# Queries stored by rows and turned by transposing DMAs, keys held as their high part twice with the low part passed through memory: one transformer layer on one Trainium2 core

## The chip, the core and the metric

The kernel is one program on one core of a Trainium2 chip. The core has a matrix engine (TensorE, PE in the profile, with its weight loads as PEld), a vector engine (VectorE, DVE), an activation engine (ScalarE, ACT), a general engine (GpSimd, POOL) and a queue engine (SyncE, SP), which here issues nearly every DMA. Each engine works through its own instructions in the order in which they were written and waits on semaphores for the others. All DMAs of the core share 16 DMA engines. SBUF is the on-chip memory, 128 partitions wide; PSUM is the small memory into which TensorE writes.

The metric is the device time of one execution in microseconds (us): less is better.

## The reference, cut to what matters

The layer takes 2048 latent rows and 256 context rows of width 1024. It normalises them, projects them with `w_in` to retention inputs (rq, rk, rv, rg) and attention inputs (aq, ak, av), runs a bidirectional retention and a dense attention side by side, projects both back with `w_out`, and ends with a squared-ReLU feed-forward part and a norm. What the change touches is the attention's queries and keys:

```
rq, rk, rv, rg, aq, ak, av = jnp.split(h @ w_in, SPLIT_IDX, axis=-1)
q = _apply_rope(_rmsnorm(aq.reshape(B, L, ATT_HEADS, ATT_HD), q_norm_g), *att_cs)
k = _apply_rope(_rmsnorm(ak.reshape(B, L, ATT_KV_HEADS, ATT_HD), k_norm_g), *att_cs)
kc = _rmsnorm(cak.reshape(B, Lc, ATT_KV_HEADS, ATT_HD), k_norm_g)
...
def _dense_attention(q, k, v):
    s = jnp.einsum('bqkgd,bskd->bkgqs', q, k).astype(jnp.float32) * ATT_SCALE
    p = jax.nn.softmax(s, axis=-1).astype(v.dtype)
    return jnp.einsum('bkgqs,bskd->bqkgd', p, v)
```

There are 8 query heads of width 64 and 2 key heads, so each key head serves a group of 4 query heads. The keys are 256 context rows and 2048 latent rows.

## The kernel before

**Stages.** The program has three stages, one after the other. The first (us 0 to 605 of the profile) normalises the rows and makes all projections; it writes the finished pieces to scratch tensors in device memory. The second (605 to about 1450) runs attention, the retention and the output projection woven together. The third is the feed-forward part.

**Float32 through two half-width parts.** TensorE multiplies float16 here, so most operands are split into a high part (the value rounded to float16) and a low part (what the rounding left), and a product is the sum of high times high, high times low and low times high. For scores that is done inside one matmul of 128 rows: a head is only 64 wide, so the 128 rows of a tile hold two things of 64 rows each.

**The layout of the scores before.** `ks` (line 138) holds, for each of the 2 key heads and all 2304 keys, the high part of the keys on rows 0 to 63 and the low part on rows 64 to 127. A query tile `qr` (128 x 2 x 4 x 128: a first half x = 0 and a second half x = 1, 4 heads, 128 queries) holds in half 0 the high part of the queries twice, so that `ks` against half 0 gives (key high + key low) x query high. Half 1 holds the low part of the queries on rows 0 to 63, and rows 64 to 95 are overwritten with the row maxima (line 204). `ks2` (lines 1520 to 1523) holds the high part of the keys on rows 0 to 63 and a constant pattern `unit` on rows 64 to 127, so that `ks2` against half 1 gives key high x query low and subtracts the maximum. `scores` (line 206) does both matmuls for a block of 128 keys; `piece` (line 172) does matmuls with `ks` and half 0 alone, from which `maximum` (line 183) takes the row maxima beforehand.

**The order of the first stage.** The projections are cut into units: one unit is one tile of 128 rows times one block of columns (RQ, RK, RV, RG, AQ of 512 columns, AKV of 256). The list (line 1186) goes through two groups of row tiles: first 2 context and 4 latent tiles, each kind of column after the other, then the other 12 latent tiles with the blocks [RV], [RK, AKV], [AQ, RQ], [RG], in which the two kinds of a block alternate. Unit s has 24 matmuls (lines 1192 to 1194). What follows on a unit is written with `do(step, part, function)` (line 307), and `run_step(s)` (line 310) issues, right after the matmuls of unit s, all that was put down for step s, in this order of parts: hi, evac, turned, low, vec, pool, root, aux, turn, load, store. So the order on each engine and on SP's queue is written out by hand, and an instruction put down for a later step stands behind all those of the earlier ones on its engine.

**A query unit (AQ, lines 763 to 789).** Step +1: ACT copies it from PSUM (`xs`). Steps +2 and +3: norm and rotary embedding on DVE and POOL give `ys`. Step +4, part turn: TensorE turns the 128 x 512 float32 tile with four transposes (line 711) into a PSUM tile `psx`. Step +5: ACT copies it as float16 (the high part, line 782), and DVE subtracts (the low part, line 785), both into `qhl`. That tile is of the ring `zs` of two buffers, which the turned RQ and RK tiles share (line 739). Step +6: SP stores it to the scratch `aq` (line 789).

**A key unit (AKV, lines 790 to 842).** Step +4: ACT copies the key as float16 (`kh`, line 829). Step +5: DVE subtracts, so that `kn` holds the key and its low part side by side in float32 (line 832). Step +6: TensorE turns both (line 837). Step +7, part vec: DVE copies the turned tile into `ks` as float16 (line 842). There are 18 key tiles.

**Loading the queries.** One attention group is one tile of 128 queries and one key head: 32 groups, in the order of the list `order` (line 266). `Group.load` (lines 157 to 164) fetches its `qr` by four DMAs of 64 KB, each from 64 rows of `aq` to 64 partitions. The first two groups are loaded during the first stage (lines 1280 and 1281, part store of fixed steps), and their pieces run there too: group 0's pieces stand in the middle of the units' matmuls (line 1489). In the second stage time goes by events k; a group has 18 of them, its load stands 14 events before its first piece (line 1569), and SP issues it in the phase dma.

Of the kernel before, what the change touches and what calls it, by code (L numbers as in the profile page):

```python
# [13 lines left out]
F16 = mybir.dt.float16  # L14
# [42 lines left out]
def layer_kernel(ctx: ExitStack, tc: tile.TileContext, a: dict, out: bass.AP):  # L57
# [31 lines left out]
    rk_d = scratch("rk", NK, [P, 512])  # L89
    rv_d = scratch("rv", NK, [P, 512])  # L90
    rg_d = scratch("rg", NT, [P, 512])
    aq_d = scratch("aq", NT, [P, 2, 4, P], F16)
    qt_d = scratch("qt", NT, [P, 512])
    kt_d = scratch("kt", NT, [P, 512])
    av_d = dram.tile([P, 2, NK, HD], F32, name="av", tag="av")
# [53 lines left out]
    class Group:  # L149
# [7 lines left out]
        def load(self):  # L157
            pool, tag = (mq, "mb") if self.n % 4 < 2 else (qp, "qr")
            self.qr = pool.tile([P, 2, 4, P], F16, name="qr", tag=tag, bufs=2)
            q = self.qr.rearrange("p x (j e) t -> p x j e t", e=2)  # L160
            for e in range(2):
                src = aq_d[self.t][64 * e : 64 * e + 64, :, 2 * self.g : 2 * self.g + 2]
                nc.sync.dma_start(q[:64, :, :, e], src)
                nc.sync.dma_start(q[64:, :, :, e], src)

        def minima(self, pool):
            if pool is None:
# [102 lines left out]
    with ExitStack() as st, tc.manual_schedule():  # L270
# [418 lines left out]
        def post(s, g, col, kind, i, x):  # L689

            row = i if kind == "c" else i + NC
            scale = RSC if col == C_RK else 1.0
            if g:
                n = 3 if col == C_RK else 4 if col == C_RG else 2
                scale = sci[:, n : n + 1]

            def evac(func=AF.Copy, width=512):
                x["x"] = new("xs", "xs", 3)
                nc.scalar.activation(x["x"][:, :width], x["ps"][:, :width], func, scale=scale)

            def new_y():
                x["y"] = new("ys", "ys", 3)
                return x["y"]

            def heads(v, h):
                return v.rearrange("p (h d) -> p h d", h=h)

            def turn():
                x["pt"] = psT.tile([P, 4, P], F32, name="psx", tag="psx")
                for h in range(4):  # L710
                    nc.tensor.transpose(x["pt"][:, h], x["y"][:, h * P : (h + 1) * P], ident)

            if col in (C_RQ, C_RK):
                do(s + 1, "evac", evac)
                if kind == "c":
                    do(s + 2, "store", lambda: nc.sync.dma_start(rk_d[row], x["x"]))
                    return

                def load():
                    x["tb"] = op.tile([P, 2, P], F32, name="rtb", tag="rtb", bufs=3)  # L720
                    nc.sync.dma_start(x["tb"], a["ret_cs"][i * P : (i + 1) * P])

                do(s, "load", load)
                rope(
                    s + 2,
                    x,
                    lambda: heads(new_y(), H),
                    lambda: heads(x["x"], H),
                    lambda: x["tb"][:, 0],
                    lambda: x["tb"][:, 1],  # L730
                    H,
                    CH,
                )
                if col == C_RK:
                    do(s + 4, "store", lambda: nc.sync.dma_start(rk_d[row], x["y"]))
                dst = qt_d[i] if col == C_RQ else kt_d[i]

                def turned():
                    x["z"] = op.tile([P, 4, P], F32, name="zs", tag="zs")
                    nc.scalar.activation(x["z"], x["pt"], AF.Copy)  # L740

                late = s + 4 + (s < 5)
                do(late, "turn", turn)
                do(late + 1, "turned", turned)
                do(late + 2, "store", lambda: nc.sync.dma_start(dst.rearrange("p (h t) -> p h t", h=H), x["z"]))
            elif col == C_RV:
                do(s + 1, "evac", evac)
                do(s + 2, "store", lambda: nc.sync.dma_start(rv_d[row], x["x"]))
            elif col == C_RG:

                def gated():
                    nc.gpsimd.tensor_tensor(new_y(), x["x"], gnb, op=ALU.mult)

                def greatest():
                    nc.vector.tensor_reduce(
                        wmx[:, 72 + i : 73 + i], x["y"], axis=AX.X, op=ALU.max, apply_absolute_value=True
                    )

                do(s + 1, "evac", evac, AF.Silu)
                do(s + 2, "pool", gated)  # L760
                do(s + 3, "vec", greatest)
                do(s + 3, "store", lambda: nc.sync.dma_start(rg_d[i], x["y"]))
            elif col == C_AQ:
                att_tables(s, x, i)
                do(s + 1, "evac", evac)
                head_norm(s + 1, x, 8, "q", scale)
                rope(
                    s + 2,
                    x,
                    lambda: heads(new_y(), 8),  # L770
                    lambda: heads(x["x"], 8),
                    lambda: x["tb"][:, 0, 0],
                    lambda: x["tb"][:, 0, 1],
                    8,
                    HD,
                    lambda: bc(x["r"].unsqueeze(2), [P, 8, HD]),
                )
                do(s + 4, "turn", turn)

                def high():  # L780
                    x["z"] = op.tile([P, 2, 4, P], F16, name="qhl", tag="zs")
                    nc.scalar.activation(x["z"][:, 0], x["pt"], AF.Copy)

                def low():
                    nc.vector.tensor_tensor(x["z"][:, 1], x["pt"], x["z"][:, 0], op=ALU.subtract)

                do(s + 5, "turned", high)
                do(s + 5, "vec", low)
                do(s + 6, "store", lambda: nc.sync.dma_start(aq_d[i], x["z"]))
            else:  # L790
                do(s + 1, "evac", evac, AF.Copy, 256)
                src = lambda: x["x"][:, 128:256].rearrange("p (g d) -> p g d", g=2)
                do(s + 2, "store", lambda: nc.sync.dma_start(av_d[:, :, row], src()))
                head_norm(s + 1, x, 2, "k", scale)

                def new_k():
                    x["kn"] = op.tile([P, 2, 2, HD], F32, name="kn", tag="kn", bufs=4)
                    return x["kn"][:, :, 0]

                r = lambda: bc(x["r"].unsqueeze(2), [P, 2, HD])  # L800
                if kind == "c":

                    def plain():
                        w = bc(g2[:, 1, 0].unsqueeze(1), [P, 2, HD])
                        nc.gpsimd.tensor_tensor(new_k(), heads(x["x"][:, :128], 2), w, op=ALU.mult)

                    do(s + 2, "pool", plain)
                    do(
                        s + 3,
                        "vec",  # L810
                        lambda: nc.vector.tensor_tensor(x["kn"][:, :, 0], x["kn"][:, :, 0], r(), op=ALU.mult),
                    )
                else:
                    att_tables(s, x, i)
                    rope(
                        s + 2,
                        x,
                        new_k,
                        lambda: heads(x["x"][:, :128], 2),
                        lambda: x["tb"][:, 1, 0],  # L820
                        lambda: x["tb"][:, 1, 1],
                        2,
                        HD,
                        r,
                    )

                def high():
                    x["kh"] = op.tile([P, 2, HD], F16, name="kh", tag="kh")
                    nc.scalar.activation(x["kh"], x["kn"][:, :, 0], AF.Copy)

                def low():
                    nc.vector.tensor_tensor(x["kn"][:, :, 1], x["kn"][:, :, 0], x["kh"], op=ALU.subtract)

                def turn_k():
                    x["pt"] = psT.tile([P, 4, P], F32, name="psx", tag="psx")
                    for g in range(2):
                        nc.tensor.transpose(x["pt"][:, g], x["kn"][:, g].rearrange("p a b -> p (a b)"), ident)

                do(s + 4, "hi", high)
                do(s + 5, "low", low)  # L840
                do(s + 6, "turn", turn_k)
                do(s + 7, "vec", lambda: nc.vector.tensor_copy(ks[:, :, row * P : (row + 1) * P], x["pt"][:, :2]))

        def value_parts(s):

# [673 lines left out]

    ks2 = vp.tile([P, 2, NK * P], F16, name="ks2")  # L1520
    for g in range(2):
        nc.sync.dma_start(ks2[:64, g], ks[:64, g])
        nc.sync.dma_start(ks2[64:, g], a["unit"])
    mts = [vp.tile([P, 4, 32], F16, name=f"mt{i}") for i in range(2)]
    for mt in mts:
# [961 lines left out]
```

## Time and profile before

| What | Value |
|---|---|
| median of 3 runs | 2648.01 us (2645.45 to 2649.12) |
| the profiled execution: its own time | 2648.93 us |
| the profiled execution: its span, first to last instruction | 2647.1 us |
| mean granted TensorE clock | 0.997 |
| bytes moved by DMA | 481.84 MB, mean 182 GB/s |
| the 64 + 64 loads of `qr`, to landing | 2.3 / 3.7 / 8.1 us (least, median, most) |
| the 16 stores of `aq`, to landing, median | 3.3 us |

The profile shows one execution. Times of instructions are from the start of the span. A group of the profile names the line of the kernel, the engine and the operation, then what it writes and reads (`qr<-aq` is a DMA that writes the tile `qr` from `aq`). "Idle before" is how long the engine stood still ahead of an instruction, with what released it. SPq rows are DMA issues on SP's queue, not the transfers. The chain of waits is followed backwards from the last instruction: at each step to what released it, or else to the instruction before it on the same engine. A view by windows gives the busy time of each engine in a stretch, then the granted clock, the share of time that the DMA engines were busy, and GB/s. Matmuls are pipelined, so their durations overlap: four transposes that take 0.60 us by their durations stand 0.44 us apart from what follows.

### The profile page before, as it was taken

What the parts mean: (1) busy time and instruction counts of PE and PEld (TensorE: products, weight loads), DVE (VectorE), ACT (ScalarE), POOL (GpSimd) and SP (SyncE); (2) the same over time, 40 slices, a digit from 0 to 9 for tenths busy, and PEclk for the clock granted to TensorE, in tenths of its full rate; (3) what the DMA queues carried; (4) which work ended last, traced back from release to release, by engine and by line L of the source; (5) the groups of instructions that cost most, each with busy time, mean ns of one, the idle gap of its engine ahead of it and who ended that gap; (6) DMA issues with size and microseconds to landing.
All of it is one profiled execution on the core that took longest, in us unless ns stands there. A gap on an engine that the chain in (4) does not pass through costs nothing.

```text
span 2647.1 us, 45439 instructions
## 1 busy us (share of the span) xinstructions
PE 2597.4 (98%) x16617; PEld 1452.3 (55%) x16617; DVE 2048.4 (77%) x3098; ACT 1504.0 (57%) x2544; POOL 1756.4 (66%) x1451
## 2 busy tenths in 40 slices
PE   8999999998999999999999999999999999999998
PEld 5875555545666666666666444444444444444443
DVE  5788898667888888888887697889886656656686
ACT  3855343426877777888788576666665322222243
POOL 3644566545676668798887685677662666666686
PEclk9999999999999999999999999999999999999999
DMA  7876999737112123333322755777685757475453
GB/s 235 270 253 211 309 325 322 261 116 221 51 57 73 57 85 100 95 85 107 112 81 77 278 160 151 236 237 230 211 291 148 278 174 296 163 288 178 157 189 113
DMA packets 332903, 481.84 MB, mean 182 GB/s; under 512 B 90228, under 2 KB 200068, under 8 KB 328200
## 3 DMA queue, kind: packets, MB, share of 16 engines
q1 hardware_dynamic: 332664, 478.94, 54.9%
q8 instruction: 130, 2.13, 0.3%
q14 instruction: 93, 0.76, 0.1%
q10 hardware_dynamic: 16, 0.01, 0.0%
HBM read 321.89 MB, written 156.38 MB: 181 GB/s over the span
## 4 chain that ended last, share of the span: by engine, by line
PE 82%; DVE 6%; DMA 4%; ACT 4%; issue 2%; POOL 2%; SPq 0%; ACTq 0%; DVEq 0%; POOLq 0%
PE pd L2298 7%; PE pd L2300 7%; PE pd L2299 7%; PE pu L2071 7%; PE pu L2073 7%; PE pu L2072 7%; PE st L210 4%; PE o L245 4%; PE st L211 4%; PE pso L1193 4%; PE pso L1192 4%; PE pso L1194 4%; PE mp L177 3%; PE o L243 2%; PE bank L1835 2%; PE bank L1833 2%
## 5 line engine op out<-in xcount | busy, mean ns | idle before, releaser
L190 DVE TENSOR_REDUCE nm<-mp 128x1 f32<-128x512 f32 x558 | 377.5, 685 | 88.6 <-PE mp L177 82.9
L216 ACT ACTIVATE p<-st 128x512 f32<-128x512 f32 x576 | 341.4, 600 | 158.4 <-PE st L211 154.8
L227 POOL TENSOR_TENSOR plo<-p,phi 128x1024 f16<-128x1024 f32 x160 | 347.7, 2178 | 84.9 <-ACT phi L220 84.8
L2071 PE MATMUL pu<-hf,w1f 128*128 128x512 f16 x896 | 339.8, 379 | 0.6 <-DVE u L1870 0.6
L2072 PE MATMUL pu<-hf,w1f 128*128 128x512 f16 x896 | 339.8, 379 | 0.0
L2073 PE MATMUL pu<-hf,w1f 128*128 128x512 f16 x896 | 339.8, 379 | 0.0
L2298 PE MATMUL pd<-w,uf 128*128 128x512 f16 x896 | 339.6, 379 | 0.0
L2299 PE MATMUL pd<-w,uf 128*128 128x512 f16 x896 | 339.6, 379 | 0.0
L2300 PE MATMUL pd<-w,uf 128*128 128x512 f16 x896 | 339.6, 379 | 0.0
L2318 POOL TENSOR_TENSOR y<-y,d 128x512 f32<-128x512 f32 x128 | 210.4, 1646 | 146.9 <-ACT uf L2287 100.1
L220 ACT ACTIVATE phi<-p 128x1024 f16<-128x1024 f32 x288 | 305.2, 1060 | 0.0
L229 DVE TENSOR_TENSOR plo<-p,phi 128x512 f16<-128x512 f32 x256 | 237.6, 929 | 21.8 <-ACT phi L220 9.4
L243 PE MATMUL o<-wv,plo 128*128 128x65 f16 x2304 | 230.6, 193 | 0.0
L245 PE MATMUL o<-wv,phi 128*128 128x129 f16 x2176 | 228.9, 220 | 0.0
L210 PE MATMUL st<-qr,ks 128*128 128x512 f16 x576 | 218.3, 379 | 10.3 <-ACT p L216 7.9
L243 PEld LDWEIGHTS <-plo 128*128 128x128 f16 x2304 | 205.5, 98 | 29.3 <-issue 1.5
L2310 DVE SCALAR_TENSOR_TENSOR y<-pd,scy,y 128x512 f32<-128x512 f32 x160 | 116.8, 747 | 131.5 <-PE pd L2300 131.5
L211 PE MATMUL st<-qr,ks 128*128 128x512 f16 x576 | 218.5, 379 | 0.0
L2083 DVE TENSOR_TENSOR r<-pu,r 128x512 f32<-128x512 f32 x224 | 149.9, 683 | 82.8 <-PE pu L2073 57.7
L1192 PE MATMUL pso<-wf,h_l 128*128 128x512 f16 (+1 forms) x576 | 208.1, 361 | 0.0
L1194 PE MATMUL pso<-wf,h_l 128*128 128x512 f16 (+1 forms) x576 | 208.1, 361 | 0.0
L1193 PE MATMUL pso<-wf,h_l 128*128 128x512 f16 (+1 forms) x576 | 208.1, 361 | 0.0
(392 smaller groups left out, 6110.4 us busy)
## 6 DMA issues: line engine op xcount, KB each, us to landing
wm<-in_w_ff SPq DMA_DIRECT2D x64, 512.0 KB, 7.1
u<-r SPq DMA_DIRECT2D x128, 256.0 KB, 4.5
ur<-u SPq DMA_DIRECT2D x128, 256.0 KB, 5.8
y<-x SPq DMA_DIRECT2D x64, 512.0 KB, 6.0
wf<-w2f SPq DMA_DIRECT2D x112, 256.0 KB, 3.0
w<-wf SPq DMA_DIRECT2D x28, 1024.0 KB, 10.2
w1r<-in_w_ff SPq DMA_DIRECT2D x48, 512.0 KB, 5.4
x<-y SPq DMA_DIRECT2D x48, 512.0 KB, 2.6
```

The lines of the kernel that those rows point to most:

```text
L190: nc.vector.tensor_reduce(dst, src, axis=AX.X, op=ALU.max, negate=True)
L211: mm(ps, ks2[:, self.g, k], q[:, 1], start=False, stop=True)
L216: nc.scalar.activation(self.p[kt // 2][:, kt % 2], self.s.pop(kt), AF.Exp, scale=HD**-0.5)
L227: nc.gpsimd.tensor_tensor(lo, p, hi, op=ALU.subtract)
L243: mm(o[:, : HD + 1], lo[:, i, c], v[:, : HD + 1], start=False, stop=False)
L245: mm(o, hi[:, i, c], v[:, :VW], start=False, stop=last)
L2071: mm(pu[hf, i], whi, hi, start=k == 0, stop=False)
L2072: mm(pu[hf, i], whi, lo, start=False, stop=False)
L2073: mm(pu[hf, i], wlo, hi, start=False, stop=k == 3)
L2298: mm(ps, u[:, 0, b], w[:, b, 0], start=b == 0, stop=False)
L2299: mm(ps, u[:, 0, b], w[:, b, 1], start=False, stop=False)
L2300: mm(ps, u[:, 1, b], w[:, b, 0], start=False, stop=b == 3)
```

## The change

The queries are no longer turned on TensorE. A query unit splits `ys` as it stands, by rows: ACT writes the high part and DVE the low part into `qhl`, now laid out as rows x 8 heads x (high, low) x 64, and SP stores it in the same place of its queue as before. The loading of a group is two transposing DMAs of 128 x 512 float16, one for each half of `qr`; both read the same 512 columns, so both halves get the high part of the queries on rows 0 to 63 and the low part on rows 64 to 127.

The keys are rearranged to match. Before they are turned, ACT copies the key beside itself in float32, so after the turn the high part stands on both halves of the rows of `ks`: `ks` against half 0 is key high x (query high + query low). DVE makes the low part after the turn, from PSUM, into a tile `kl` with a single buffer, which SP stores to a scratch `kl` in device memory. `ks2` gets its rows 0 to 63 from that scratch, so `ks2` against half 1 is key low x query high; the rows of the maxima stand where they stood.

```diff
--- before.py
+++ after.py
@@ -89,7 +89,8 @@
     rk_d = scratch("rk", NK, [P, 512])
     rv_d = scratch("rv", NK, [P, 512])
     rg_d = scratch("rg", NT, [P, 512])
-    aq_d = scratch("aq", NT, [P, 2, 4, P], F16)
+    aq_d = scratch("aq", NT, [P, 2, 4 * P], F16)
+    kl_d = dram.tile([HD, 2, NK, P], F16, name="kl", tag="kl")
     qt_d = scratch("qt", NT, [P, 512])
     kt_d = scratch("kt", NT, [P, 512])
     av_d = dram.tile([P, 2, NK, HD], F32, name="av", tag="av")
@@ -157,11 +158,8 @@
         def load(self):
             pool, tag = (mq, "mb") if self.n % 4 < 2 else (qp, "qr")
             self.qr = pool.tile([P, 2, 4, P], F16, name="qr", tag=tag, bufs=2)
-            q = self.qr.rearrange("p x (j e) t -> p x j e t", e=2)
-            for e in range(2):
-                src = aq_d[self.t][64 * e : 64 * e + 64, :, 2 * self.g : 2 * self.g + 2]
-                nc.sync.dma_start(q[:64, :, :, e], src)
-                nc.sync.dma_start(q[64:, :, :, e], src)
+            for x in range(2):
+                nc.sync.dma_start(self.qr[:, x], aq_d[self.t][:, self.g], transpose=True)
 
         def minima(self, pool):
             if pool is None:
@@ -775,18 +773,20 @@
                     HD,
                     lambda: bc(x["r"].unsqueeze(2), [P, 8, HD]),
                 )
-                do(s + 4, "turn", turn)
 
                 def high():
-                    x["z"] = op.tile([P, 2, 4, P], F16, name="qhl", tag="zs")
-                    nc.scalar.activation(x["z"][:, 0], x["pt"], AF.Copy)
+                    x["z"] = op.tile([P, 8, 2, HD], F16, name="qhl", tag="zs")
+                    nc.scalar.activation(x["z"][:, :, 0], heads(x["y"], 8), AF.Copy)
 
                 def low():
-                    nc.vector.tensor_tensor(x["z"][:, 1], x["pt"], x["z"][:, 0], op=ALU.subtract)
+                    nc.vector.tensor_tensor(x["z"][:, :, 1], heads(x["y"], 8), x["z"][:, :, 0], op=ALU.subtract)
+
+                def store():
+                    nc.sync.dma_start(aq_d[i].rearrange("p g n -> p (g n)"), x["z"].rearrange("p h a d -> p (h a d)"))
 
                 do(s + 5, "turned", high)
                 do(s + 5, "vec", low)
-                do(s + 6, "store", lambda: nc.sync.dma_start(aq_d[i], x["z"]))
+                do(s + 6, "store", store)
             else:
                 do(s + 1, "evac", evac, AF.Copy, 256)
                 src = lambda: x["x"][:, 128:256].rearrange("p (g d) -> p g d", g=2)
@@ -824,22 +824,24 @@
                         r,
                     )
 
-                def high():
-                    x["kh"] = op.tile([P, 2, HD], F16, name="kh", tag="kh")
-                    nc.scalar.activation(x["kh"], x["kn"][:, :, 0], AF.Copy)
-
-                def low():
-                    nc.vector.tensor_tensor(x["kn"][:, :, 1], x["kn"][:, :, 0], x["kh"], op=ALU.subtract)
+                def double():
+                    nc.scalar.activation(x["kn"][:, :, 1], x["kn"][:, :, 0], AF.Copy)
 
                 def turn_k():
                     x["pt"] = psT.tile([P, 4, P], F32, name="psx", tag="psx")
                     for g in range(2):
                         nc.tensor.transpose(x["pt"][:, g], x["kn"][:, g].rearrange("p a b -> p (a b)"), ident)
 
-                do(s + 4, "hi", high)
-                do(s + 5, "low", low)
+                def parts():
+                    pt, hi = x["pt"][:, :2], ks[:, :, row * P : (row + 1) * P]
+                    x["kl"] = op.tile([HD, 2, P], F16, name="kl", tag="kl", bufs=1)
+                    nc.vector.tensor_copy(hi, pt)
+                    nc.vector.tensor_tensor(x["kl"], pt[:HD], hi[:HD], op=ALU.subtract)
+
+                do(s + 4, "hi", double)
                 do(s + 6, "turn", turn_k)
-                do(s + 7, "vec", lambda: nc.vector.tensor_copy(ks[:, :, row * P : (row + 1) * P], x["pt"][:, :2]))
+                do(s + 7, "vec", parts)
+                do(s + 7, "store", lambda: nc.sync.dma_start(kl_d[:, :, row], x["kl"]))
 
         def value_parts(s):
 
@@ -1519,7 +1521,7 @@
 
     ks2 = vp.tile([P, 2, NK * P], F16, name="ks2")
     for g in range(2):
-        nc.sync.dma_start(ks2[:64, g], ks[:64, g])
+        nc.sync.dma_start(ks2[:64, g], kl_d[:, g].rearrange("d n t -> d (n t)"))
         nc.sync.dma_start(ks2[64:, g], a["unit"])
     mts = [vp.tile([P, 4, 32], F16, name=f"mt{i}") for i in range(2)]
     for mt in mts:
```

## The prediction

> **What bounds the kernel now.** I read the page's span and engine lines first, then busy time by windows, cut where the chain of waits changes hands, then the chain itself.
>
> ```profile
> span 2647.1 us, 45439 instructions
> PE 2597.4 (98%) x16617; PEld 1452.3 (55%) x16617; DVE 2048.4 (77%) x3098; ACT 1504.0 (57%) x2544; POOL 1756.4 (66%) x1451
> PE 82%; DVE 6%; DMA 4%; ACT 4%; issue 2%; POOL 2%; SPq 0%; ACTq 0%; DVEq 0%; POOLq 0%
> 326.00:424.00 98.00, 92.62 (x532) 52.31 (x529) 92.52 (x127) 44.44 (x78) 65.72 (x73) 1.00 0.97 345
> 424.00:514.00 90.00, 89.60 (x475) 48.22 (x476) 66.44 (x110) 34.29 (x61) 54.59 (x58) 1.00 0.80 259
> 514.00:553.00 39.00, 37.29 (x191) 19.04 (x188) 30.35 (x62) 11.88 (x18) 21.45 (x20) 1.00 0.55 186
> 605.00:1450.00 845.00, 828.43 (x7912) 551.84 (x7912) 729.66 (x1335) 671.17 (x1114) 647.40 (x559) 1.00 0.31 92
> ```
>
> TensorE is the bound: 98% busy, 82% of the chain. The columns of a window are its length, then busy time of PE, PEld, DVE, ACT and POOL, the clock, the DMA share and GB/s. From 424 to 514, where query and retention-query units alternate, PE is busy 89.6 of 90 us. From 326 to 424, where key units run, DVE is as full as PE, and the DMA engines are at 0.97. Attention (605 to 1450) does the same matmuls after the change; only its loads differ. So the change is decided in the first 640 us.
>
> **1. The turns that go away.** In the chain the query turns from 424 to 514 are the first of each pair (a query unit, then a retention one); the last query turn stands at 552.
>
> ```profile
> 424.40 0.66 PE psx L711 x4
> 436.75 0.44 PE psx L711 x4
> 512.69 0.44 PE psx L711 x4
> 552.24 0.63 PE psx L711 x4
> ```
>
> The first and last of eight stand at 424.40 and 512.69, one each 12.6 us. They are worth 0.66 + 7 x 0.44 = 3.7 us where PE sets the end, and the one at 552.24 another 0.6: -4.4 in all. The other seven lie where DVE or a DMA also holds the end, and I give them nothing. All sixteen would be 16 x 0.44 = 7.0, so the term lies between -7.0 and 0.
>
> **2. The queries' two parts, and the keys' low part.** The counts stay; the sources move.
>
> ```profile
> L785 DVE TENSOR_TENSOR qhl<-psx,qhl x16: 675/691/693, 125.3 to 559.7; 128x512 f16<-128x512 f32 x16
> L832 DVE TENSOR_TENSOR kn<-kn,kh x18: 270/284/812, 97.6 to 411.5; 128x128 f32<-128x128 f32 x18
> L842 DVE CAST ks<-psx x18: 405/411/425, 101.4 to 423.9; 128x256 f16<-128x256 f32 x18
> L635 DVE TENSOR_TENSOR t<-xs,rtb x32: 677/1209/2841, 71.6 to 552.0; 128x512 f32<-128x512 f32 x32
> ```
>
> Figures are least, median and most in ns. A subtraction from PSUM (line 785) is always near 691; the DVE instruction of the same size with its inputs in SBUF (line 635) takes 677 to 1209 and more. The new one reads SBUF: 0 to +0.53 each. Some two of them lie on DVE's part of the chain (514 to 553): +1.1. The key's new subtraction is as large as the copy beside it (64 x 256 out of PSUM, 411) and replaces one of 284: +0.13 each, about 7 of them between 326 and 424: +0.9. Together +2.0, between 0 and 18 x 0.13 + 16 x 0.53 = +10.8. ACT's two copies change only their operands, and ACT is under half busy there.
>
> **3. The low keys' store and its single buffer.** This is a new wait in two places. DVE's next subtraction waits until the last tile's store has landed, and SP, whose queue runs ahead of DVE, now stops at that store until DVE has come.
>
> ```profile
> 104.05 0.52 SPq L793 DMA_DIRECT2D av<-xs  x1
> 105.14 0.42 DVE L842 CAST ks<-psx 128x256 f16<-128x256 f32 x1
> 112.26 3.75 DVE L541 TENSOR_TENSOR wlo<-wst,whi 128x1024 fp32r<-128x1024 f32 x3 [4.42 <-issue]
> 116.14 0.41 DVE L842 CAST ks<-psx 128x256 f16<-128x256 f32 x1
> 119.25 0.42 DVE L842 CAST ks<-psx 128x256 f16<-128x256 f32 x1
> 162.81 8.80 DMA wmo<-in_w_mod
> av<-xs SPq DMA_DIRECT2D x18, 64.0 KB, 5.4
> 305.64 0.33 SPq L745 DMA_DIRECT2D kt<-zs  x1
> 310.69 0.41 DVE L842 CAST ks<-psx 128x256 f16<-128x256 f32 x1
> 318.54 0.41 DVE L842 CAST ks<-psx 128x256 f16<-128x256 f32 x1
> ```
>
> For the store's landing I take that of `av` (5.4): it also goes in runs of 256 bytes, in the same steps. In the first row group the store of the first key tile stands where `av` is issued, 104.05, and lands at 109.5. The second tile's subtraction could start at 105.14 + 0.42 = 105.6: 3.9 us of wait, inside the 4.42 us that DVE stands idle before 112.26. The third is written at 116.14 + 0.8 = 116.9 and lands at 122.3, and the fourth wants the buffer at 119.7: 2.6 us that nothing hides. Behind it on DVE stand the retention scales and low parts, and in the end the release of the buffer for the load at 162.81 that the chain passes through. So +2.6, between 0 and 3.9 + 2.6 = 6.5. In the second row group the tiles come 7.85 us apart (310.69, 318.54), longer than 5.4 plus the copy, so DVE does not wait. SP does: its place for the store is at 305.64, and it stands there until 311.4. The loads behind it come up to 5.8 us later, yet they serve the step after the next, some 10 us on: +0.5, between 0 and 5.8.
>
> The Trainium skill says in "DMA: Bandwidth & Descriptors", section Rules for kernel authors, that transfers under 64 KB are mostly overhead and should be coalesced. The store of 32 KB is such a one, the 5.4 us of a 64 KB store agree, and by that rule the 18 should be one; the sum would be 3.1 lower.
>
> **4. The transposing loads.** No row of before is of this kind. Four loads of 64 KB become two of 128 KB, with the same bytes.
>
> ```profile
> L163 SPq DMA_DIRECT2D qr<-aq x64: 573/612/1142, 453.2 to 1373.9; - x64
> DMA to landing us min/median/max: 2.3/3.7/8.1
> 453.17 0.65 SPq L163 DMA_DIRECT2D qr<-aq  x1
> 455.44 0.61 SPq L164 DMA_DIRECT2D qr<-aq  x1
> 459.12 0.38 PE L1194 MATMUL pso<-wf,h_l 128*128 128x512 f16 x1
> 459.34 0.38 PE L177 MATMUL mp<-ks,qr 128*128 128x512 f16 x1
> 903.24 0.58 SPq L163 DMA_DIRECT2D qr<-aq  x1
> 931.84 0.33 SPq L1850 DMA_DIRECT2D x<-xr  x1
> 956.46 0.58 SPq L163 DMA_DIRECT2D qr<-aq  x1
> ```
>
> At best a transpose is a plain load: 453.17 + 0.6 + 0.6 + 3.7 = 458.1, before the first piece at 459.34, no loss. At worst one takes the longest landing of these loads, 8.1 us, and holds its queue for it: 453.17 + 16.2 = 469.4, a stall of PE of 10.0. I take 5.4 each, one after the other, again the row that moves 256-byte pieces under a busy stage (a 128-wide block of a row is 256 bytes): landed at 464.0, PE stalls 4.6. PE had no gap there (459.12, 459.34), so it is lost in full. SP leaves its fourth load at 456.05 now and would leave the second transpose at 464.0; the loads and the `qt` store behind it come 8 us later here and again for group 1, which the PSUM ring of five buffers mostly takes up: +1, between 0 and 8.
>
> In attention the same is hidden. Two groups are 956.46 - 903.24 = 53.2 us, 36 events of 1.48; the load stands 14 events, 20.7 us, ahead, and SP issues nothing from there to 931.84. Two transposes of 10.3 each would still be in time.
>
> The skill's "VectorE: DVE Perf Modes", section The three transpose paths, gives 1.309 us for a DMA transpose of 128 x 128. As an estimate, eight blocks a group would be 10.5 us against my 10.8; no row here shows it, and the sum would be the same to 0.4.
>
> **5. The start of attention.**
>
> ```profile
> 602.78 0.61 SPq L163 DMA_DIRECT2D qr<-aq  x1
> 608.09 0.55 SPq L1619 DMA_DIRECT2D orv<-rv  x1
> 612.62 4.91 DMA sf<-sf
> L1522 SPq DMA_DIRECT2D ks<-ks x2: 532/657/782, 579.6 to 580.8; - x2
> L211 PE MATMUL st<-qr,ks x576: 377/379/634, 603.6 to 1453.4; 128*128 128x512 f16 x192
> ```
>
> Group 2's load stands in front of the retention's loads at 608.09, and the retention's states are on the chain (612.62). SP would be through at 602.8 + 10.8 = 613.6, up to 5.5 later. Those loads run some events ahead: +2, between 0 and 5.5. The load of `ks2` moves to device memory; issued at 579.6 for a first use at 603.6 it has 24 us, so nothing.
>
> **Sum.** -4.4 + 2.0 + 2.6 + 0.5 + 4.6 + 1 + 2 = +8.3. The profiled execution took 2648.9 (span 2647.1 and 1.8 around it), 0.9 above the median of the runs, so it would come to 2657.2 and the median to 2656.3. I forecast 2656: slower by 0.3%. What a measurement here can tell from no change is about 0.2%, 5.3 us.
>
> **The rivals.**
> A, not slower: the transposes land like the loads they replace (the 3.7 us row) and the low keys' wait is hidden. The mechanism is TensorE's shorter list; it decides once a pair of transposes lands within 459.34 - 453.17 = 6.2 us. Then terms 3 to 5 vanish, DVE has room for term 2, and the turns count: -4.4 and three more of the first row group at 0.44, 2642.3; with all sixteen 2641. For it: PE at 89.6 of 90. Against it: the DMA share, 0.80 to 0.97, in which little lands at its least.
> B, no change: transposes of 4 us each, landed at 461.2 (stall 1.8), term 3 half hidden, the rest of 4 and 5 small: about -4.4 + 2.0 + 1.5 + 1.8 + 1 = +2, 2650.
> C, a transpose holds SP for 8 us or more in the full stages: stall 10.0, both queue terms at their ends (8 and 5.5): +8.3 + 5.4 + 7 + 3.5 = 24, 2672. For it: SP issues in order, and the whole first stage is fed from it.
> D, the transposes take over 10.3 us: then the cover in attention is gone too, and each of 30 groups stalls PE; at 12 each, 30 x 3.3 = 99 us, 2750. A transposing DMA that goes element by element would end there or above. Against it: the plain loads' 3.7.
>
> **How the numbers follow.** Forecast 0.40, A 0.24, B 0.22, C 0.10, D 0.04. The range 2642 to 2674 leaves out D, the end of C and what lies below A. Slower by over 0.2% (above 2653.3): C, D, 0.34 of the forecast and 0.02 of B, 0.50; faster (below 2642.7): 0.20 of A; within: 0.30. The forecast's own range, with its terms a little off, is 2650 to 2664.
>
> **What would show it.** Right: no turn of a query in the first stage; a gap of PE ahead of group 0's first piece, with the transposing load as its releaser; DVE waiting for the store of `kl` once or twice between 105 and 125; SP standing at that store in each second step after 300; no wait of PE for `qr` after 640. Wrong: pieces that start without a gap (A or B), gaps at every group (D), or a first stage that becomes longer between 180 and 420, where I charge 1.4 us.

## The result, and the profile after

The changed kernel takes 2655.2 us (median of 7 runs, 2651.8 to 2656.4) against 2648.0 (7 runs, 2643.5 to 2650.1): ratio 1.0029, 95% interval 1.002 to 1.0038. It is slower by 0.3%. The forecast was 2656, but two groups of its terms were badly off, in opposite directions.

The page of the changed kernel, its span and engines, and the shares of its chain of waits:

```profile
span 2654.6 us, 45165 instructions
PE 2594.8 (98%) x16553; PEld 1445.6 (54%) x16553; DVE 2056.2 (77%) x3098; ACT 1505.4 (57%) x2544; POOL 1767.3 (67%) x1451
PE 79%; DVE 6%; DMA 6%; ACT 4%; POOL 2%; issue 2%; SPq 1%; DVEq 0%; POOLq 0%; ACTq 0%
```

TensorE has 64 instructions fewer, the sixteen query turns of four, and 2.6 us less work, yet the span grew by 7.5. The chain has 3% less of TensorE and 2% more of DMA, which points to time lost ahead of TensorE, in loads.

Where? Some DVE instructions are the same in both kernels, one per unit of the second row group, and serve as marks: the first sum of squares of a key, the last copy of a key tile, the last sum of squares of a query. These are the three rows for the kernel before, then for the changed one; the two times in a row are the first and the last start.

```profile
L664 DVE TENSOR_REDUCE hs_k<-sq x12: 272/274/280, 285.3 to 394.9; 128x2 f32<-128x128 f32 x12
L842 DVE CAST ks<-psx x18: 405/411/425, 101.4 to 423.9; 128x256 f16<-128x256 f32 x18
L664 DVE TENSOR_REDUCE hs_q<-sq x12: 671/673/680, 401.0 to 544.0; 128x8 f32<-128x512 f32 x12
```

```profile
L662 DVE TENSOR_REDUCE hs_k<-sq x12: 272/273/280, 288.1 to 400.0; 128x2 f32<-128x128 f32 x12
L838 DVE CAST ks<-psx x18: 403/412/425, 100.8 to 431.0; 128x256 f16<-128x256 f32 x18
L662 DVE TENSOR_REDUCE hs_q<-sq x12: 672/674/680, 405.8 to 551.6; 128x8 f32<-128x512 f32 x12
```

The changed kernel is 2.8 us late at the first mark, 7.1 at the second and 7.6 at the third; its end is 7.5 late. So the net change arose before 552: 2.8 before 285, 4.3 from there to the last key tile (the "key stretch", 138.6 us before), and 0.5 in the "query stretch" (120.1 before), where the missing turns should have brought a gain. What follows the third mark is 0.1 shorter in all: 0.3 longer up to the first score matmul, 3.0 shorter from the first to the last score matmul (850.0 before, 847.0 after), 2.6 longer from there to the end. `plain_loads`, an experiment below without the transposing loads, has the same 847.0, so they are not what shortens it; why these two parts moved was not tried.

In the key stretch SP, the queue that feeds the first stage, tells the story. These are rows of its stands from 285 to 450 (us in total, times, longest): first the kernel before, then the changed one.

```profile
SPq L1152 <- PE psf L1160: 20.6, 4, 7.0
```

```profile
SPq L844 <- DVE kn L646: 12.8, 4, 7.7
SPq L844 <- DVE kl L839: 6.5, 4, 1.8
SPq L1154 <- DMA wm<-in_w_ff: 1.4, 2, 0.8
```

Before, SP's largest item was 20.6 us at the early retention loads, waiting for TensorE: that is its lead. After, it stands 19.3 us (12.8 + 6.5) at the store of the low keys (line 844), waiting for DVE to come to that tile, and at the early loads (now line 1154) it no longer waits for TensorE in this window: the lead is gone. The order of its issues shows what stands behind that store; again the kernel before, then the changed one (selected rows):

```profile
303.07 0.56 SPq L916 DMA_DIRECT2D wm<-in_w_ff  x1
305.64 0.33 SPq L745 DMA_DIRECT2D kt<-zs  x1
306.49 0.48 SPq L369 DMA_DIRECT2D wmo<-in_w_mod  x1
312.48 0.48 SPq L916 DMA_DIRECT2D wm<-in_w_ff  x1
```

```profile
305.81 0.77 SPq L918 DMA_DIRECT2D wm<-in_w_ff  x1
314.17 0.53 SPq L844 DMA_DIRECT2D kl<-kl  x1
314.80 1.07 SPq L743 DMA_DIRECT2D kt<-zs  x1
316.39 0.45 SPq L367 DMA_DIRECT2D wmo<-in_w_mod  x1
319.73 0.47 SPq L918 DMA_DIRECT2D wm<-in_w_ff  x1
```

The store comes first among its step's DMAs. The `kt` store behind it leaves 9.2 us later than before (305.64, 314.80), the weight loads 9.9 (306.49, 316.39) and 7.3 (312.48, 319.73). Of that 2.8 was there at the first mark; the stand itself makes 6.4, 7.1 and 4.5. What this does can be seen on the chain of the changed kernel, from the end of the key stretch into the query stretch (the longest DMA pieces: start, length, what):

```profile
429.79 9.19 DMA early<-rk
440.31 7.44 DMA wm<-in_w_ff
447.77 5.09 DMA wm<-in_w_ff
465.56 7.03 DMA wm<-in_w_ff
472.65 5.12 DMA aq<-qhl
```

In the kernel before the chain was on TensorE without a break from 424 to 514; here it runs over loads until 487. The same window in both, before first:

```profile
430.00:470.00 40.00, 40.00 (x212) 21.07 (x210) 27.61 (x43) 15.92 (x29) 23.15 (x25) 1.00 0.90 288
```

```profile
430.00:470.00 40.00, 36.45 (x171) 17.51 (x170) 31.77 (x48) 13.30 (x24) 24.38 (x24) 0.91 0.86 289
```

TensorE did nothing for 3.55 us of the 40, and its mean granted clock in the window (a share of full speed) is 0.91, where it was 1.00.

The transposing loads, on which the prediction put the largest term, are no trouble:

```profile
L162 SPq DMA_TRANSPOSE qr<-aq x64: 1188/1262/2071, 461.1 to 1378.6; - x64
DMA to landing us min/median/max: 2.5/3.1/7.1
461.10 2.85 SPq L162 DMA_TRANSPOSE qr<-aq  x2
466.95 0.38 PE L175 MATMUL mp<-ks,qr 128*128 128x512 f16 x1
```

One takes 1.26 us of SP, two 2.85, against 2.9 for the four plain loads before (453.17 to 456.05), and it lands after 3.1 us (median of all), not later than the 3.7 of a plain one. Group 0's first piece starts 5.9 us after the first issue, with no gap of TensorE in front of it; before it was 6.2.

### The profile page after: what moved, and what is told of

Its sections match the earlier page's. It is cut to its first block, busy times and chain, and to the rows that moved or that the text cites. A ratio compares the mean times of both kernels' runs of the same rounds, so it can differ in the third digit from the quotient of the medians.

```text
span 2654.6 us, 45165 instructions
## 1 busy us (share of the span) xinstructions
PE 2594.8 (98%) x16553; PEld 1445.6 (54%) x16553; DVE 2056.2 (77%) x3098; ACT 1505.4 (57%) x2544; POOL 1767.3 (67%) x1451
## 4 chain that ended last, share of the span: by engine, by line
PE 79%; DVE 6%; DMA 6%; ACT 4%; POOL 2%; issue 2%; SPq 1%; DVEq 0%; POOLq 0%; ACTq 0%
PE pd L2302 7%; PE pd L2300 7%; PE pd L2301 7%; PE pu L2073 7%; PE pu L2074 7%; PE pu L2075 7%; PE st L208 4%; PE o L243 4%; PE st L209 4%; PE mp L175 3%; PE pso L1195 3%; PE pso L1194 3%; PE pso L1196 3%; PE o L241 2%; PE bank L1837 2%; PE bank L1835 2%
```

## The experiments

Each was timed against the kernel before in five rounds. The two stretches are read from one profiled execution of each, by the marks above, and given as the difference in us from the kernel before. Left out of the table are the time ahead of the first mark, since it varies between -0.6 and +6.6 us over these executions, and is +6.5 in one that has no store to wait for (`one_store_only`), and what follows the third mark (-0.9 to +3.7). With one execution each, a microsecond in a stretch is no finding.

```
kernel              ratio   95% interval       key stretch  query stretch
changed             1.0029  1.0020 to 1.0038   +4.3         +0.5
two_halves          1.0034  1.0021 to 1.0046   +4.5         +0.1
plain_loads         1.0035  1.0022 to 1.0048   +5.3         +0.3
late_one_buffer     1.0037  1.0025 to 1.0050   +6.9         -6.1
turns_back          1.0039  1.0027 to 1.0052   +4.1         +5.5
store_late          1.0009  1.0000 to 1.0018   +1.9         -4.8
late_turns_back     1.0026  1.0016 to 1.0036   +0.5         +4.5
one_store_only      0.9992  0.9984 to 1.0001   +0.4         -4.2
late_twice          1.0035  1.0022 to 1.0049   +5.5         +0.4
late_from_act       1.0002  0.9994 to 1.0011   +1.0         -4.2
late_wide           1.0006  0.9996 to 1.0016   +1.1         -3.0
late_wide_act       1.0004  0.9995 to 1.0012   +0.4         -5.6
late_double_turns   1.0082  1.0068 to 1.0095    0.0        +14.8
```

**The place of the store.** Both halves of a transposed key tile hold the same values, so a second buffer needs no room: odd tiles take the low part from the upper 64 partitions.

```
@@ parts(), with klt = [] ahead of post()
-  x["kl"] = op.tile([HD, 2, P], F16, name="kl", tag="kl", bufs=1)
+  n = len(klt)
+  klt.append(klt[0] if n else op.tile([P, 2, P], F16, name="kl", tag="kl", bufs=1))
+  h = slice(HD * (n % 2), HD * (n % 2) + HD)
+  x["kl"] = klt[0][h]
   nc.vector.tensor_copy(hi, pt)
-  nc.vector.tensor_tensor(x["kl"], pt[:HD], hi[:HD], op=ALU.subtract)
+  nc.vector.tensor_tensor(x["kl"], pt[h], hi[h], op=ALU.subtract)
```

> Theory G (the place of the store): of the 7.5 us that the span grew, 2.5 come from DVE's waits for the store of the low keys before 165, and 4 to 5 from SP, which stands at that store for 19.3 us in all between 295 and 470, so that the weight loads behind it leave some 8 us later. Rival T (the traffic): the 18 stores of 256-byte pieces lengthen the loads of a stage whose DMA engines are at 0.97. Here the low keys alternate between the two halves of one tile, and the store stays in its place. DVE's two waits (5.2 us) go, SP stands as before. G and T: 2.5 us less than the changed kernel, 2652.7, ratio 1.0018. If the stage is fed by loads anyway, so that the time gained is lost again at the next weight load: 2655, ratio 1.0029.

DVE's two waits, 5.2 us in the changed kernel, are gone, and nothing is won: 1.0034 against 1.0029, with the 1.0018 of the first case just outside the interval. SP stands 18.9 us at the store, as long as in the changed kernel, and the key stretch is as long (+4.5):

```profile
SPq L849 <- DVE kn L646: 14.6, 5, 7.7
SPq L849 <- DVE kl L844: 4.3, 3, 2.1
```

This is the second case of the expectation, that of a stage fed by loads. The profiled execution took 2652.4 us, the least of its five (to 2658.4), so its span of 2650.6 says little; the median decides.

The second edit moves the store one step, with the two halves (`store_late`), and with the single buffer (`late_one_buffer`):

```
-  do(s + 7, "store", lambda: nc.sync.dma_start(kl_d[:, :, row], x["kl"]))
+  do(s + 8, "store", lambda: nc.sync.dma_start(kl_d[:, :, row], x["kl"]))
```

> The two halves, and the store one step later, when its product is there: neither DVE nor SP stands. The traffic is the same. G: 2.5 + 4 to 5 less, 2648 to 2649, ratio 1.000; and where TensorE then sets the end from 424 to 514 again, the turns that went away show too, down to 2644.5, ratio 0.9987. T: only DVE's waits go, 2652.7, ratio 1.0018.

1.0009: by the ratios 0.0020 x 2648 = 5.3 us come back, with the same traffic. The interval (1.0000 to 1.0018) does not touch that of the changed kernel. Both stretches answer: +1.9 in place of +4.3, and -4.8 in place of +0.5. The marks of `store_late`:

```profile
L662 DVE TENSOR_REDUCE hs_k<-sq x12: 271/273/280, 284.7 to 395.2; 128x2 f32<-128x128 f32 x12
L843 DVE CAST ks<-psx x18: 406/411/425, 100.2 to 425.3; 128x256 f16<-128x256 f32 x18
L662 DVE TENSOR_REDUCE hs_q<-sq x12: 670/674/680, 401.1 to 540.6; 128x8 f32<-128x512 f32 x12
```

From 425.3 to 540.6 are 115.3 us, where the kernel before needs 120.1: here the missing turns show. SP's stand at the store from 285 to 450 has shrunk from 19.3 us to little more than 5.1, and it waits for TensorE at the early loads again, though less than the 20.6 of the kernel before:

```profile
SPq L1159 <- PE psf L1167: 8.5, 4, 6.3
SPq L849 <- DVE kn L646: 5.1, 2, 4.6
```

A part of the 5.3 us in the query stretch is the clock: its mean is 1.00 there, in the changed kernel 0.97, and the same matmuls keep TensorE busy for 112.1 us in place of 113.8.

> The store one step later with the single buffer kept: SP does not stand, DVE waits longer (a store that leaves about 3 us after its product and lands 6.3 later, against key tiles 3 to 8 us apart). G: SP's 4 to 5 us come back, DVE's waits in the first row group grow by 3 to 8 and in the second stand at 1 or so each: 2651 to 2658. T: nothing comes back and DVE's waits add, 2658 or more.

1.0037. The row of DVE's waits in this kernel (total, times):

```profile
  DMA kl<-kl: 21.2, 7
```

What SP gains, DVE loses at the buffer: 21.2 us of waits in place of 5.2, about half of them in each row group. Where the loss comes in cannot be read from its one execution: +6.9 and -6.1 in the stretches, +6.6 ahead of the first mark. The later store pays only with the second buffer; the two edits that bring 5.3 us together bring nothing one by one.

**What the store costs where nobody stands.** `one_store_only` stores one tile's low part and spreads it over all eighteen in the later load; `late_twice` issues each late store a second time into other memory.

```
@@ one_store_only
-  do(s + 7, "store", lambda: nc.sync.dma_start(kl_d[:, :, row], x["kl"]))
+  last.append(row)
+  if len(last) == NK:
+      do(s + 8, "store", lambda: nc.sync.dma_start(kl_d[:, :, 0], x["kl"]))
```

> Leaves out 17 of the 18 stores of the low keys; the second score tile takes the last tile's low part for all eighteen. Nothing stands at a store and nothing of it moves. T (the traffic of the stores costs what the late store still leaves): 2 to 4 less than the late store, 2643 to 2645, ratio 0.9985 to 0.9993. G (the place alone was the cost): within 1.5 of the late store, 2645.5 to 2648, ratio 0.9995 to 1.0013.

> The two halves and the late store (1.0009), each store issued a second time into memory that nothing reads. Leaving 17 of 18 out gave 0.9992, so if a store in a place where nobody stands still costs (its traffic and SP's issue), eighteen more cost the same again, 4.5 us: ratio 1.0026. If that difference was chance, as the intervals allow (they touch at 1.000): up to 1 us more, ratio 1.0009 to 1.0013.

Without the stores 0.9992, with them 1.0009, with twice as many 1.0035. The first step is 4.5 us, and its intervals just overlap; the second is 6.9, and its intervals lie apart. So theory T has its share: a store in its later place still costs some 0.25 to 0.4 us (4.5 and 6.9 over 18). The first step is not quite free of stands, since `one_store_only` also takes away the 5.1 us that SP still stands in `store_late`; the second is cleaner, with 4.6 of that left in `late_twice`. Whether a store costs by its bytes, its pieces or SP's issue was asked next, on top of `store_late`: 512-byte pieces (`late_wide`), ScalarE's queue (`late_from_act`), and both. In the excerpts the later load of the low keys, rearranged to match the wide store, is left out.

```
@@ late_wide
-  kl_d = dram.tile([HD, 2, NK, P], F16, name="kl", tag="kl")
+  kl_d = dram.tile([NK, HD, 2 * P], F16, name="kl", tag="kl")
...
-  nc.sync.dma_start(kl_d[:, :, row], x["kl"])
+  nc.sync.dma_start(kl_d[row], x["kl"].rearrange("d g t -> d (g t)"))
@@ late_from_act
-  nc.sync.dma_start(kl_d[:, :, row], x["kl"])
+  nc.scalar.dma_start(kl_d[:, :, row], x["kl"])
```

> The late store with the low keys kept in memory tile by tile, so that a store moves 64 pieces of 512 bytes in place of 128 of 256; the later load of the second key tile takes the small pieces instead, at 580, where it has 24 us. If the stores' cost goes by pieces: half of 4.5 less, ratio 1.0000. If it goes by bytes or by SP's issue: as the late store, 1.0009.

> The two halves, the store one step later and issued by ScalarE's queue, which also has work at less than half its time there. If SP's own issuing (18 stores of 0.53, 9.6 us over both row groups) still holds the weight loads: 2 less than the late store, 2645, ratio 1.000. If not: 2646 to 2648, ratio 1.0005 to 1.0013. If ScalarE stands at the store instead: 1 to 3 more, 2648 to 2650.

> The wide pieces and ScalarE's queue together: the candidate that should beat both kernels. Late store 1.0009, by ScalarE's queue 0.7 thousandths less, by wide pieces up to 0.9 less: 0.9993, 2646. If neither change was more than chance: 1.0005 to 1.001.

1.0006, 1.0002 and 1.0004, each within the others' intervals and that of `store_late`. Which part of a store costs stays open. None of them beats the kernel before; they are level with it.

**The turns.** The four transposes of each query unit on TensorE are put back into a PSUM tile that nothing reads:

```
+  do(s + 4, "turn", turn)
   do(s + 5, "turned", high)
```

> The changed kernel with the sixteen query turns put back on TensorE, into a PSUM tile that nothing reads: the price of term 1 in the changed kernel. Term 1 as the prediction has it (TensorE sets the end from 424 to 514 and at 552): 4.4 more, 2659.6, ratio 1.0045. Theory G (SP standing at the store, so that this stage waits for its weight loads; TensorE was busy 36.45 of 40 us from 430 to 470): the turns fall into TensorE's idle time, 0 to 1.5 more, 2655 to 2656.7, ratio 1.003 to 1.0036.

> The same turns put back on top of the two halves and the later store (2646.9). If the wait of SP was what hid the saving of the turns: 4.4 more, 2651.3, ratio 1.0026; with all sixteen on the path 7, 2653.9. If the turns lie beside other work there too: 2647 to 2648, ratio 1.0009 to 1.0013.

On the late store: 1.0026 - 1.0009 = 0.0017, 4.5 us, as term 1 has it. In the changed kernel: 1.0039 - 1.0029 = 0.0010, 2.6 us, between the two expectations, with intervals that hold both; that SP's stand hides a part of the saving is likely, not shown. The query stretch grows in both when the turns come back: +0.5 becomes +5.5, -4.8 becomes +4.5. The second step, 9.3, is more than the prediction's 7.0 for all sixteen turns, so it is not the turns alone: the granted clock of that stretch is 0.97 in `late_turns_back` and 1.00 in `store_late`.

**The transposing loads.** `plain_loads` takes the four plain loads a group, `late_double_turns` issues each transposing load twice on top of `store_late`.

```
@@ late_double_turns
   nc.sync.dma_start(self.qr[:, x], aq_d[self.t][:, self.g], transpose=True)
+  nc.sync.dma_start(self.qr[:, x], aq_d[self.t][:, self.g], transpose=True)
```

> The changed kernel with the four plain loads a group in place of the two transposing ones: the same bytes, the queries in another order, so the scores are of other pairs. Term 4 of the prediction (transposes of 5.4 us each, a stall of TensorE of 4.6 and 1 for the queue): 5.6 less, 2649.6, ratio 1.0006. G, by which the transposes are like the loads they replace (landing 3.1 against 3.7 median): within 1 us of the changed kernel, 2654 to 2656, ratio 1.0025 to 1.0031.

1.0035, and 1.0006 lies outside its interval: the transposes show no cost against plain loads. Term 4 falls.

> The late store with every transposing load issued twice: four of 1.26 us of SP a group in place of two. If the transposes stand on the path at group 0 and group 1 (term 4): the second pair brings 2.5 us each, ratio 1.0009 + 0.0019 = 1.003. If their landing is covered (in the first stage by the steps ahead, in attention by the 20.7 us that the load is ahead): 0 to 1 us, ratio 1.0009 to 1.0013. If the cover in attention is gone at four: 30 groups of 1 or more, 30 us, ratio 1.012.

1.0082, 0.0073 x 2648 = 19 us above `store_late`: none of the three. The copy writes the same tile as its original, so SP stands until that has landed. From SP's timeline at the first two groups (selected rows):

```profile
456.73 1.42 SPq L162 DMA_TRANSPOSE qr<-aq  x1
460.37 1.19 SPq L163 DMA_TRANSPOSE qr<-aq  x1
464.47 1.19 SPq L163 DMA_TRANSPOSE qr<-aq  x1
465.72 0.57 SPq L722 DMA_DIRECT2D rtb<-in_ret_cs  x1
491.13 1.94 SPq L162 DMA_TRANSPOSE qr<-aq  x1
498.27 1.19 SPq L163 DMA_TRANSPOSE qr<-aq  x1
503.54 0.58 SPq L924 DMA_DIRECT2D wm<-in_w_ff  x1
```

and four of the waits from 465 to 520 (total, times, longest):

```profile
ACT zs L741 <- DMA qt<-zs: 21.9, 4, 12.9
ACT qhl L782 <- DMA aq<-qhl: 16.9, 3, 11.6
PE mp L176 <- ACT xs L700: 7.6, 1, 7.6
PE pso L1200 <- ACT sq L658: 4.2, 1, 4.2
```

SP is taken for 9.0 us at group 0 and 12.4 at group 1, where a pair takes 2.8 and 3.9 in `store_late`: 14.7 us more. The `aq` and `qt` stores behind leave late, ScalarE finds no free buffer of the ring that `zs` and `qhl` share, and TensorE stands. As at the store, SP stands and what it issues behind comes late, in another place and at a dearer price: the query stretch grows from -4.8 to +14.8. Of that, 6.5 us are TensorE's own: it is busy 118.6 us there, against 112.1, at a granted clock of 0.94. In attention, waits for the loads are not what a second pair costs: of the waits of all engines for data of `qr`, this is what falls to the loads, the first stage included.

```profile
  DMA qr<-aq: 1.1, 2
```

Yet from the first to the last score matmul this execution takes 852.9 us, where `store_late` takes 847.6; what those 5.3 us are was not tried.

## Why the prediction was right, and where it was not

By the ratios, in us: the place of the store, with its single buffer, +5.3 (`store_late`), the stores themselves +4.5 (`one_store_only`), the turns -4.5 (`late_turns_back`), and what is left of 1.0029, +2.4. Each difference has an uncertainty of more than 3 us.

**Term 1, the turns, -4.4.** About right in size: 4.5 on the late store, 2.6 in the changed kernel, though their uncertainty allows zero for the second and all sixteen turns (7.0) for the first. The path is less sure. The term counted turns where TensorE sets the end; on the chain of `store_late` from 424 to 552 the `aq` stores (14.0%) and the `wm` loads (10.9%) come first, and no TensorE line is among the first ten.

**Term 2, the sources, +2.0.** The subtraction of the queries from SBUF, before and after (count, then busy us and mean ns in all):

```profile
L785 DVE TENSOR_TENSOR qhl<-psx,qhl 128x512 f16<-128x512 f32 x16 | 11.0, 687 | 37.3 <-ACT qhl L782 37.3
```

```profile
L782 DVE TENSOR_TENSOR qhl<-ys,qhl 128x512 f16<-128x512 f32 x16 | 11.5, 722 | 35.7 <-ACT qhl L779 35.7
L839 DVE TENSOR_TENSOR kl<-psx,ks 64x256 f16<-64x256 f32 x18 | 7.5, 417 | 5.8 <-DMA kl<-kl 5.2
```

The queries' ones grew by 0.035 us each, not by the 0.53 that was put down; the key's one takes 417, where 411 was put down in place of 284. So as durations the term comes to about 1.0 in place of 2.0: the keys' 0.9, and less than 0.1 for the queries. What the left +2.4 is was not tried; it is less than the uncertainty.

**Term 3, the store.** The waits came where they were forecast. The chain of the changed kernel goes through them:

```profile
120.60 0.42 DVE kl L839
121.43 6.33 DMA kl<-kl
```

and landing took 6.3, not 5.4. DVE waited 3.8 and 1.4 us, where 3.9 (hidden) and 2.6 were worked out. But their worth was the wrong way round. DVE's waits were given 2.6: taking them away alone returned nothing. SP's stand was given 0.5, because the loads behind it "serve the step after the next, some 10 us on": this is the step that failed. The delay of up to 5.8 us was roughly right for one stand (4.5 to 7.1 in the rows above). But it was set once against a lead of 10 and found harmless, where the stands come back, 19.3 us of them from 285 to 450, and spend the lead that SP had built, 20.6 us of stands at the early loads; by 440 the weight loads are on the chain. The store also has a price in a place where hardly anyone stands, which the term left out. 3.1 in all was forecast, 5.3 + 4.5 = 9.8 came. The sign to watch was named rightly: a first stage that becomes longer between 180 and 420.

**Terms 4 and 5, the transposes, +5.6 and +2.** Wrong; here the half of rival A that lets the transposes land like plain loads held, while its other half, that the low keys' wait is hidden, did not. Their duration was taken from the `av` store's row, the nearest one with 256-byte pieces: that is the step of term 4 that failed. Landing went like the plain loads' (3.1 against 3.7), TensorE had no gap at group 0, and no wait for the loads showed in attention. For term 5, no more than 0.3 us shows from the third mark to the first score matmul (59.4 before, 59.7 after). The Trainium skill gives 1.309 us for a DMA transpose of 128 x 128 bf16 in "VectorE: DVE Perf Modes", section The three transpose paths; a load here has four such blocks, of f16, and lands in 3.1 us median, 0.8 a block with all that lies between issue and landing, so here the figure cannot be multiplied by the blocks, as the prediction's sentence on it did. Rival C gave 16 us above the forecast to a queue held for 8 us or more by each transpose. `late_double_turns`, where a group's four loads hold SP for 9.0 and 12.4 us, is 19 above `store_late`: a like size, but by another path, late `aq` and `qt` stores, so it is no test of C.

So the total was right by luck: 7.6 us too much on the transposes stood against 6.7 too little on the store. The rule of the Trainium skill that was quoted beside term 3 ("DMA: Bandwidth & Descriptors", section Rules for kernel authors: small transfers are mostly overhead) agrees with the landing times: 6.3 us for these 32 KB, no less than the `av` store's 64 KB (5.4 before, 4.8 after). Whether the same bytes in fewer stores would cost less than the 4.5 us of these 18 was not tried; fewer, larger pieces within each store could not be told apart from chance.

## What to carry to other kernels

A store put into a queue that also issues the loads should not come before its product: here a queue that ran ahead gave up its lead to the engine that it waited for, and the loss turned up far behind, as late weight loads. So when a change adds a DMA to such a queue, count first how long the queue will stand there each time, add that up over all steps, and set the sum against the lead that the queue has (its stands at work that comes later), not one stand against one lead. Place the store after its product, and give it the second buffer that this needs in the same edit: here each alone brought nothing.

## What the runs showed of the hardware

A transposing load of four 128 x 128 blocks of f16 takes 1.26 us of the issuing queue where a plain load of half its bytes takes 0.61, and it lands no later (3.1 us median against 3.7). Eighteen stores of 32 KB in a place where SP hardly stands cost 4.5 to 6.9 us, in a stretch whose DMA engines are busy at 0.93 (the key stretch of `store_late`). The granted clock of the query stretch differs between the kernels: 1.00 in `store_late`, 0.97 in the changed kernel and 0.94 in `late_double_turns`, where TensorE is idle for 3.3, 6.8 and 16.3 us; but it is 0.97 in `late_turns_back` too, with 2.8 us idle, so idle time there does not explain it alone. The start of the profiled executions differs by 7 us without following what the kernels do: the first mark of the second row group came at 284.7 in `store_late` and at 291.8 in `one_store_only`, though the latter does less, so that stretches between marks say more than the span.
